# Transposing queries and keys before they are split, with three smaller changes of order, in one diffusion trunk layer

## The chip, the cores and the metric

The kernel runs on one core of a Trainium2 chip. The core has five engines that run their own instruction queues and meet at semaphores: TensorE (PE in the profile; PEld is its weight load), VectorE (DVE), ScalarE (ACT), GpSimd (POOL), and SyncE (SP), which here only issues transfers. The metric is the device time of one execution in microseconds; the median of several runs is given.

## The reference

One trunk layer is computed for 256 prompt tokens and 1024 latent tokens of width 1024, in fp32:

```
h = rms_norm(x) * (1 + sc1) + sh1          # sc, sh, g from an adaLN of the conditioning
z = h @ w_in                               # 5376 columns
  q, k = per-head RMSNorm (8 query heads, 2 key heads of 64); latents also get 2-D rotary positions
  attention: latents read 512 cached keys + 1024 latent keys, the prompt reads itself
  HGRN2: gated linear recurrence, both directions, 4 heads of 128
merged = sigmoid(g0) * (o_h @ w_ho) + sigmoid(g1) * (o_a @ w_ao)
x = x + g1 * (merged @ w_out)
h = rms_norm(x) * (1 + sc2) + sh2
x = x + g2 * (square(relu(h @ w_ff1)) @ w_ff2)
y = rms_norm(x) * final_norm_w
```

It returns y for prompt and latents, the prompt's normalised keys and its values, and the final recurrent states.

## The kernel before

**Split products.** PE multiplies in a reduced format (fp32r) at a higher rate than plain fp32. For accuracy each operand is split into a high half (a copy rounded to fp32r, made by ACT) and a low half (the rest, subtracted by DVE); a product is then three matmuls: high x high, high x low, low x high. The helper is `split` at L276 to L278, so L277 is always ACT's copy and L278 always DVE's subtraction, whatever the tile. Queries and keys are stacked: a tile of 128 partitions holds 64 rows of the high half over 64 of the low half, so that one matmul with a key tile that holds its high half twice, and one with its low half twice, give the score (L699).

**Stages, in order of time.** (1) Conditioning and the input's norm, then queries of the second group of heads, keys and values: for each of three token tiles (512, 512 and 256 tokens) and each of eight 128-wide slices of the width, the input is transposed (`norm1_tr`, L256), scaled into high and low halves (`norm1_col`: L265 and L270 on ACT, L271 on DVE), and multiplied (`front_z`, L563, L564, L567). (2) Queries of the first group (`z_tok`). (3) Attention, with other columns of w_in as filler between its steps. (4) The recurrence, with the merge gates as filler. (5) Branch outputs, merge, output projection. (6) The first FFN product of the prompt (L1361 to L1383, matmuls L306 to L308): 16 pairs of 128 columns; beside it the sums of the latents are made (`sums1`, L1343). (7) The first FFN product of the latents, with a scheme of seven block products instead of eight (L1442 on); the sums of products are taken by DVE. (8) The second FFN product, in seven chains, the last one P3, and the final norm, whose last blocks come after the chain.

**Queries and keys (L383 to L487).** When a pair of 128-token blocks is projected, `qk_norm` normalises it and, for latents, rotates it. `k_stack` and `q_consume` then split each block in token order (`kst` L419/L420, `qst` L473/L474), and put a function `late` on a list. `late` transposes four 128 x 128 pieces on PE (L425, L479), copies the PSUM tile out on ACT (`kT` L428, `qT` L482) and stores it to scratch memory (KS, QS), from where attention loads K and Q tiles (`Kl`, `Ql`). For keys both halves are written twice, so that each tile is loaded whole. `kT` and `qT` share a ring of two buffers (G); normalised queries and keys lie in rings of three (D, E); the split copies have a ring of four (B). The PSUM ring `t` has two buffers and serves the input's transposes and these.

**What sets the order.** PE's instructions run in the order in which they are written. When a `late` runs is decided by `due` and `flush`: a small clock of DVE's work, to which each item adds a constant (`DUE`), against one of PE's; `flush` is called between steps of PE. From stage 6 on SP is in written order too. The order of ACT, DVE and POOL (and SP before) is written by the framework's planner, which simulates the program by its own cost estimates and gives a free engine the ready instruction that is earliest in the program. `tc.high_priority(offset=n)` makes it count n places earlier. The order is then fixed for the run. In stage 6 a weight block of 1 MB comes into one of two buffers (`wraw`), is split by `w_oc` under offset 150 into a ring of six (`wsp`), and the product is squared by `relu2` under offset 400.

**The last norm.** `square` sums the squares of half a row block on ACT (L1675); `final` (L1677) forms the reciprocal root with POOL (L166) and scales each half by it and by the norm's weight in one DVE instruction (L1685), then stores it.

## Time and profile before

| what | value |
|---|---|
| median of 3 runs | 2084.43 us (2083.12 to 2084.66) |
| profiled execution, its own time | 2085.25 us |
| its span | 2083.5 us |
| granted TensorE clock, mean | 0.995 |
| PE busy | 97% of the span |

The profile gives for each group of instructions the line of the program, the engine, the tiles as out<-in, their shape and count, the busy time and mean duration, and the idle time of the engine just before them with what ended it. In the order of time a row begins with its start and its duration in us. A matmul's duration contains its latency; matmuls overlap, so the price of one is read from start to start.

### The profile page before, as it was taken

Reading aid. Unit: us, or ns where it says so; the run is one execution under the profiler, and the core shown is the slowest. Engines: PE = TensorE matmul, PEld = TensorE weight load, DVE = VectorE, ACT = ScalarE, POOL = GpSimd, SP = SyncE. Lnnn points to the kernel's source line nnn. Section 1 sums busy time; section 2 is a strip of 40 time slices with the busy share of each in tenths; the row PEclk is TensorE's granted clock in tenths of the full one; section 3 lists DMA queues with packets and bytes.
Section 4 is the critical chain, followed back from the end, with each engine's and each line's share of the span. In section 5 each row is a group of like instructions: output and inputs, shape, how many; then the busy total and the mean of one; then the engine's idle time right before and its main releaser. Section 6 shows DMA issues by size and latency. Waiting matters only on the chain.

```text
span 2083.5 us, 33949 instructions
## 1 busy us (share of the span) xinstructions
PE 2026.9 (97%) x12552; PEld 1747.1 (84%) x12552; DVE 1405.9 (67%) x2677; ACT 943.1 (45%) x1928; POOL 539.3 (26%) x577
## 2 busy tenths in 40 slices
PE   6899999999999999999999999999999999999998
PEld 5688889988899878888888888988888888888886
DVE  4784776777776788779354636776666666677786
ACT  4754555555555522222231425654555444333442
POOL 1472233432332355546112100222221210000010
PEclk9999999999999999999999999999999999999999
DMA  9464221241222255445644523764444479545773
GB/s 309 125 195 139 71 73 55 66 133 53 68 82 70 73 168 181 129 151 166 220 132 147 192 101 110 228 198 160 144 155 153 153 260 366 161 155 176 232 249 128
DMA packets 230246, 319.24 MB, mean 153 GB/s; under 512 B 18072, under 2 KB 148720, under 8 KB 230080
## 3 DMA queue, kind: packets, MB, share of 16 engines
q1 hardware_dynamic: 217664, 277.41, 41.4%
q0 software_dynamic: 12416, 39.66, 5.4%
q8 instruction: 99, 1.62, 0.3%
q14 instruction: 67, 0.55, 0.1%
HBM read 229.43 MB, written 87.57 MB: 152 GB/s over the span
## 4 chain that ended last, share of the span: by engine, by line
PE 84%; DVE 8%; DMA 3%; ACT 3%; issue 2%; POOL 1%; SPq 0%; DVEq 0%; POOLq 0%; ACTq 0%
PE ps_g L306 7%; PE ps_g L308 7%; PE ps_g L307 7%; PE ps_s L699 4%; PE ps_t L740 4%; PE ps_g L1593 2%; PE ps_g L1591 2%; PE ps_g L1592 2%; PE ps_s L1439 2%; PE ps_g L756 2%; PE ps_s L1441 2%; PE ps_s L1440 2%; PE ps_g L755 2%; PE ps_g L323 2%; PE ps_g L325 2%; PE ps_g L324 2%
## 5 line engine op out<-in xcount | busy, mean ns | idle before, releaser
L306 PE MATMUL ps_g<-hs,wsp 128*128 128x512 f32 (+1 forms) x896 | 323.5, 361 | 0.4 <-DVE adas L186 0.4
L308 PE MATMUL ps_g<-hs,wsp 128*128 128x512 f32 (+1 forms) x896 | 310.8, 347 | 0.8 <-DVE wsp L278 0.8
L307 PE MATMUL ps_g<-hs,wsp 128*128 128x512 f32 (+1 forms) x896 | 310.6, 347 | 0.0
L718 POOL TENSOR_SCALAR pexp<-pexp,rs 128x512 f32<-128x512 f32 (+1 forms) x104 | 170.6, 1647 | 363.0 <-ACT pTh L743 180.0
L277 ACT ACTIVATE wsp<-wraw 128x1024 fp32r<-128x1024 f32 x110 | 109.6, 998 | 260.5 <-PE ps_g L307 82.9
L278 DVE TENSOR_TENSOR wsp<-wraw,wsp 128x1024 fp32r<-128x1024 f32 x110 | 133.6, 1216 | 120.3 <-ACT wsp L277 120.0
L308 PEld LDWEIGHTS ps_g<-hs,wsp 128*128 128x128 f32 x896 | 170.2, 190 | 22.8 <-DVE wsp L278 1.0
L306 PEld LDWEIGHTS ps_g<-hs,wsp 128*128 128x128 f32 x896 | 170.2, 190 | 21.6 <-issue 4.8
L307 PEld LDWEIGHTS ps_g<-hs,wsp 128*128 128x128 f32 x896 | 170.7, 190 | 15.3
L743 ACT ACTIVATE pTh<-ps_t 128x512 fp32r<-128x512 f32 x200 | 118.8, 601 | 131.0 <-PE ps_t L740 126.7
L700 DVE TENSOR_REDUCE mx<-ps_s 128x1 f32<-128x512 f32 (+1 forms) x208 | 136.9, 663 | 49.6 <-PE ps_s L699 48.8
L277 ACT ACTIVATE ah<-ar 128x640 fp32r<-128x640 f32 (+1 forms) x112 | 81.0, 723 | 190.3 <-PE ps_g L1592 102.3
L710 ACT ACTIVATE pexp<-ps_s,ngm 128x512 f32<-128x512 f32 (+1 forms) x208 | 137.3, 669 | 42.4 <-DVE ngm L704 40.7
L278 DVE TENSOR_TENSOR ah<-ar,ah 128x640 fp32r<-128x640 f32 (+1 forms) x112 | 90.2, 805 | 81.1 <-ACT ah L277 80.4
L744 DVE TENSOR_TENSOR pTl<-ps_t,pTh 128x512 fp32r<-128x512 f32 x200 | 136.1, 681 | 11.9 <-ACT pTh L743 11.4
L699 PE MATMUL ps_s<-Kl,Ql 128*128 128x512 f32 (+1 forms) x416 | 127.8, 412 | 2.5 <-ACT pexp L710 2.5
L740 PE MATMUL ps_t<-ident,pexp 128*128 128x128 f32 x800 | 121.0, 273 | 2.5 <-DVE pexp L718 1.5
L323 PE MATMUL ps_g<-wsp,hs 128*128 128x256 f32 x400 | 117.1, 293 | 0.0
L325 PE MATMUL ps_g<-wsp,hs 128*128 128x256 f32 x400 | 113.4, 283 | 0.0
L324 PE MATMUL ps_g<-wsp,hs 128*128 128x256 f32 x400 | 113.0, 283 | 0.0
L756 PE MATMUL ps_g<-pTl,Vl 128*128 128x256 f32 x400 | 105.4, 286 | 4.0 <-DVE pTl L744 3.9
L755 PE MATMUL ps_g<-pTh,Vl 128*128 128x256 f32 x400 | 105.5, 284 | 1.3 <-DVE oa L765 1.0
(420 smaller groups left out, 5425.3 us busy)
## 6 DMA issues: line engine op xcount, KB each, us to landing
ar<-AF SPq DMA_DIRECT2D x112, 320.0 KB, 3.4
wraw<-in_w_ff SPq DMA_DIRECT2D x32, 1024.0 KB, 6.2
wr<-in_w_ff SPq DMA_DIRECT2D x128, 256.0 KB, 4.4
wraw<-in_w_in SPq DMA_DIRECT2D x18, 1024.0 KB, 5.9
wraw<-in_w_ada SPq DMA_DIRECT2D x16, 1024.0 KB, 5.5
AF<-a POOLq DMA_DIRECT2D x48, 256.0 KB, 2.7
AF<-t POOLq DMA_DIRECT2D x48, 256.0 KB, 2.3
wa<-in_w_ada SPq DMA_DIRECT2D x32, 256.0 KB, 5.8
```

The source lines that it names most:

```text
L277: s_.activation(hi, raw, AF.Copy)
L278: v.tensor_tensor(lo, raw, f32(hi), op=ALU.subtract)
L306: pe.matmul(out, hi[:, k, :], mh, start=(first and k == 0), stop=False)
L307: pe.matmul(out, hi[:, k, :], ml, start=False, stop=False)
L308: pe.matmul(out, lo[:, k, :], mh, start=False, stop=(last and k == kcs - 1))
L323: pe.matmul(po[:, bb, :], mh[:, off:off + P], wh[:, k % 4, :], start=(k == 0), stop=False)
L324: pe.matmul(po[:, bb, :], mh[:, off:off + P], wl[:, k % 4, :], start=False, stop=False)
L325: pe.matmul(po[:, bb, :], ml[:, off:off + P], wh[:, k % 4, :], start=False, stop=(k == KC - 1))
L699: pe.matmul(pq[:, 0:n], self.qh[:, q0:q0 + P], K[self.g][var][self.kts[i]], start=(var == 0), stop=(var == 1))
L718: NORM[(i + j) % len(NORM)].tensor_scalar(x, x, self.rs[j], None, op0=ALU.mult)
L740: pe.transpose(pt[:, a, j * P:(j + 1) * P], self.Ps[j][i][:, b * P:(b + 1) * P], ident)
L755: pe.matmul(pv[:, 0:256], V[self.g][kg][:, b, :], hi[:, a, :], start=(k == 0), stop=False)
```

## The change

Four things are changed.

1. Queries and keys are no longer split and stacked in token order. `late` transposes the plain fp32 tile (for a pair of blocks: four transposes for queries, two heads of 64 in each; two for keys, both key heads in each) into PSUM, and splits there: ACT copies the high half, DVE subtracts the low half from PSUM. Key halves are stored once. The loads of K and Q put the two halves together: two transfers of 64 partitions each. There is one `late` per pair where there was one per block, and the constants of `DUE` become 3.4 and 4.4.
2. In stage 6 the weight splits get an offset of 500 instead of 150.
3. In stage 7 the sum `u2` gets an offset of 100.
4. For the second half of the five row blocks that end last, POOL multiplies by the norm's weight ahead, in place, after the half's squares are summed (in chain P3). `final` then only scales this half by the reciprocal root, on ACT.

```diff
-    QS = [[DR((P, 4, n), "QS%d_%d" % (g, t)) for t, (_, n, _) in enumerate(TT)] for g in range(2)]
+    QS = [[DR((2, 2, P, n), "QS%d_%d" % (g, t)) for t, (_, n, _) in enumerate(TT)] for g in range(2)]
-    KS = [DR((P, 4, KG[kg]), "KS%d" % kg) for kg in range(4)]
+    KS = [DR((2, P, KG[kg]), "KS%d" % kg) for kg in range(4)]
...
     def k_stack(kr, kgv, pos):
-        st = S((P, 2, 2, 2, 64), F32R, name="kst")
-        kb = kr.unsqueeze(2).broadcast_to([P, 2, 2, 64])
-        s_.activation(st[:, :, 0], kb, AF.Copy)
-        v.tensor_tensor(st[:, :, 1], kb, f32(st[:, :, 0]), op=ALU.subtract)
         def late():
-            pt = PS("t", (P, 4, P))
-            for j in range(4):
-                pe.transpose(pt[:, j, :].bitcast(F32R), st[:, j // 2, j % 2].rearrange("p a d -> p (a d)"), ident_r)
-            e = S((P, 4, P), F32R, name="kT")
+            pt = PS("t", (P, 2, P))
+            for b in range(2):
+                pe.transpose(pt[:, b, :], kr[:, b].rearrange("p k d -> p (k d)"), ident)
+            e = S((P, 2, 256), F32R, name="kT")
             with tc.high_priority(offset=600):
-                s_.activation(e, pt, AF.Copy)
-            dma(KS[kgv][:, :, pos * P:(pos + 1) * P], e)
+                split(e[:, 0], e[:, 1], pt.rearrange("p b c -> p (b c)"))
+            dma(KS[kgv][:, :, pos * P:(pos + 2) * P].rearrange("v p n -> p v n"), e)
...
+            t, off = pr // 2, (pr % 2) * 256
+            def late():
+                pt = PS("t", (P, 2, 256))
+                for b in range(2):
+                    for a in range(2):
+                        pe.transpose(pt[:, a, b * P:(b + 1) * P], qr[:, b, 2 * a:2 * a + 2].rearrange("p h d -> p (h d)"), ident)
+                hi, lo = [S((P, 2, 256), F32R, name="qT") for i in range(2)]
+                with tc.high_priority(offset=600):
+                    split(hi, lo, pt)
+                for i, x in enumerate((hi, lo)):
+                    dma(QS[g][t][i, :, :, off:off + 256].rearrange("a p n -> p a n"), x)
+            pending.append((due(DUE[1]), late))
...
-    DUE = (2.2, 2.6, 6.5)
+    DUE = (3.4, 4.4, 6.5)
...
                 x = S(dt=F32R, name="Ql")
-                dma(x, QS[self.g][self.t][:, h % 4, :])
+                for i in range(2):
+                    dma(x[64 * i:64 * i + 64, :], src[i, a, r:r + 64, :])
...
-            K[g][var][kg] = S((P, KG[kg]), F32R, name="Kl")
-            dma(K[g][var][kg], KS[kg][:, 2 * g + var, :])
+            x = K[g][var][kg] = S((P, KG[kg]), F32R, name="Kl")
+            for i in range(2):
+                dma(x[64 * i:64 * i + 64, :], KS[kg][var, 64 * g:64 * g + 64, :])
...
-            with tc.high_priority(offset=150 if i > 1 else 0):
+            with tc.high_priority(offset=500 if i > 1 else 0):
                 wt = w_oc(r, half)
...
-        v.tensor_tensor(u2, Y, s1_, op=ALU.add)
+        with tc.high_priority(offset=100):
+            v.tensor_tensor(u2, Y, s1_, op=ALU.add)
...
-            v.scalar_tensor_tensor(x, x, rst[:, 0:1], fw[0][:, c], op0=ALU.mult, op1=ALU.mult)
+            if i in ready.get(b, ()):
+                s_.activation(x, x, AF.Copy, scale=rst[:, 0:1])
+            else:
+                v.scalar_tensor_tensor(x, x, rst[:, 0:1], fw[0][:, c], op0=ALU.mult, op1=ALU.mult)
...
+    ready = {}
+    def weigh(b, i):
+        x = xt[b][:, i * 512:(i + 1) * 512]
+        g_.tensor_tensor(x, x, fw[0][:, i * 512:(i + 1) * 512], op=ALU.mult)
+        ready.setdefault(b, []).append(i)
+    def square_weigh(b, i):
+        square(b, i)
+        weigh(b, i)
...
-    chain2("P3", Z, False, {2 * j + 4: lambda b=b: square(b, 1) for j, b in enumerate((4, 5, 6, 7, 9))})
+    chain2("P3", Z, False, {2 * j + 4: lambda b=b: square_weigh(b, 1) for j, b in enumerate((4, 5, 6, 7, 9))})
```

More of the change, by code (lines that the diff above doesn't have):

```diff
@@ L462, in kv_consume @@
         v_stack(vr, 2, kgv, pos)
-        for b in range(2):
-            k_stack(kr[:, b], kgv, pos + b)
+        k_stack(kr, kgv, pos)
     def q_consume(g):
@@ L468, in f @@
             _, qr = qk_norm(po.rearrange("p b (h d) -> p b h d", h=4), 4, qwb, 2 * pr, pr < 4)
-            for b in range(2):
-                blk = 2 * pr + b
-                t, off = blk // 4, (blk % 4) * P
-                st = S((P, 4, 2, 64), F32R, name="qst")
-                s_.activation(st[:, :, 0], qr[:, b], AF.Copy)
-                v.tensor_tensor(st[:, :, 1], qr[:, b], f32(st[:, :, 0]), op=ALU.subtract)
-                def late(st=st, t=t, off=off):
-                    pt = PS("t", (P, 4, P))
-                    for h in range(4):
-                        pe.transpose(pt[:, h, :].bitcast(F32R), st[:, h].rearrange("p a d -> p (a d)"), ident_r)
-                    e = S((P, 4, P), F32R, name="qT")
-                    with tc.high_priority(offset=600):
-                        s_.activation(e, pt, AF.Copy)
-                    dma(QS[g][t][:, :, off:off + P], e)
-                pending.append((due(DUE[1]), late))
+            t, off = pr // 2, (pr % 2) * 256
[10 more added lines that the diff above has]
+            pending.append((due(DUE[1]), late))
         return f
@@ L495, in cache_kv @@
             v_stack(cv[:, 2 * b:2 * b + 2], 2, 0, 2 * b)
-        for b in range(4):
-            k_stack(ck[:, b], 0, b)
+        for b in range(0, 4, 2):
+            k_stack(ck[:, b:b + 2], 0, b)
     clk = {"pe": 0.0, "dve": 0.0}
-    DUE = (2.2, 2.6, 6.5)
+    DUE = (3.4, 4.4, 6.5)
     def due(work):
@@ L777, in load_k @@
             x = S((P, 2, 256), F32R, name="Kl")
-            dma(x, KS[3][:, 2 * g:2 * g + 2, :])
+            for i in range(2):
+                dma(x[64 * i:64 * i + 64], KS[3][:, 64 * g:64 * g + 64, :].rearrange("v p n -> p v n"))
             K[g][0][3], K[g][1][3] = x[:, 0, :], x[:, 1, :]
```

6 lines of the change are left out of this document (4 added, 2 removed), and 2 rows, old and new, of the table RING_OF.

## The prediction

> **What bounds the kernel now.** I read the page first, then busy time by stretch, then TensorE's waits, then the order of time where those waits lie.
>
> ```profile
> span 2083.5 us, 33949 instructions
> ...
> PE 2026.9 (97%) x12552; PEld 1747.1 (84%) x12552; DVE 1405.9 (67%) x2677; ACT 943.1 (45%) x1928; POOL 539.3 (26%) x577
> ```
>
> TensorE (PE) is the bound nearly everywhere, so an edit pays in two ways only: fewer PE slots, or a shorter PE wait. The stretches that the edits touch:
>
> ```profile
> 92.00:112.00 20.00, 15.53 (x82) 11.74 (x80) 15.76 (x38) 16.04 (x41) 11.63 (x17) 1.00 0.51 156
> 112.00:176.00 64.00, 64.00 (x468) 59.46 (x469) 38.90 (x77) 33.54 (x75) 30.94 (x33) 1.00 0.68 208
> ...
> 1310.00:1340.00 30.00, 26.90 (x220) 26.28 (x219) 24.08 (x41) 17.20 (x33) 8.31 (x11) 1.00 0.73 227
> ...
> 1384.00:1400.00 16.00, 14.21 (x63) 11.43 (x62) 14.13 (x26) 6.81 (x12) 2.82 (x4) 1.00 0.39 118
> ```
>
> After the window come its length and the busy time of PE, weight loads, VectorE (DVE), ScalarE (ACT) and GpSimd (POOL). In 92 to 112 us, where the prompt's part of the first projection runs, PE lacks 4.5 us and ACT is busy 16 of 20; from 112 to 176 PE never rests, so there only fewer slots count. The first FFN product of the prompt lacks 3.1 us in 1310 to 1340, its hand-over to the latents 1.8 in 1384 to 1400. Who ended PE's waits (total, times, longest):
>
> ```profile
> PE ps_t L938 <- DVE usf L909: 5.7, 3, 3.0
> ...
> PE ps_s L308 <- DVE wsp L278: 2.3, 2, 1.5
> ...
> PE ps_s L1439 <- DVE u L1453: 1.8, 1, 1.8
> PE ps_s L567 <- DVE hs L271: 1.7, 1, 1.7
> ...
> PE ps_g L308 <- DVE wsp L278: 0.8, 1, 0.8
> ...
> PE ps_t L425 <- ACT qT L482: 0.5, 1, 0.5
> ```
>
> and, of the stretch 76 to 112 us alone, the group of the input's transposes:
>
> ```profile
> L256 PE MATMUL ps_t<-ident,xr 128*128 128x128 f32 x20 | 4.0, 292 | 3.4 <-ACT xnb L270 2.3 <-ACT kT L428 1.2
> ```
>
> **Transposes, PE slots.** Before, a pair of token blocks costs eight transposes of split data (fp32r) for four query heads, and eight for the keys. After, four and two of plain fp32. The keys have 7 pairs (2 cached, 5 new), the queries 10 (5 per group of heads): 136 transposes become 54. The price is read from start to start, in order of time, plain fp32 first:
>
> ```profile
> 69.78 0.60 PE L256 MATMUL ps_t<-ident,xr 128*128 128x128 f32 x4
> 70.13 0.48 PE L563 MATMUL ps_g<-wraw,hs 128*128 128x512 f32 x1
> 70.44 0.40 PE L564 MATMUL ps_g<-wsp,hs 128*128 128x512 f32 x1
> 70.68 0.40 PE L563 MATMUL ps_g<-wraw,hs 128*128 128x512 f32 x1
> ```
>
> ```profile
> 105.27 0.46 PE L479 MATMUL ps_t<-ident,qst 128*128 128x128 f32 x4
> 105.57 0.46 PE L563 MATMUL ps_s<-wsp,hs 128*128 128x512 f32 x1
> 105.87 0.39 PE L564 MATMUL ps_s<-wsp,hs 128*128 128x512 f32 x1
> ```
>
> Four plain ones take 0.35 us, and the product behind them 0.31 where the next has 0.24: 0.42 in all. Four split ones take 0.30, the product behind 0.30: 0.36. A query pair goes from 2 x 0.36 = 0.72 to 0.42, saving 0.30; a key pair from 0.72 to 0.35/2 + 0.07 = 0.25, saving 0.47. That is 10 x 0.30 + 7 x 0.47 = 6.3 us. Where two groups or another transpose follow one another, the 0.06 behind a group was paid once or not at all; on slots alone it is 10 x 0.25 + 7 x 0.42 = 5.5. I take 5.9, the middle.
>
> The Trainium skill's FP8 and Floating Point Precision (TensorE Precision Notes) speaks against this part: true fp32 takes four passes through the array. The two fences above disagree for transposes: the plain kind costs 0.35 against 0.30 for four. What four passes would do to the time is a rival below.
>
> **Transposes, other engines.** Per key or query pair:
>
> ```profile
> L428 ACT ACTIVATE kT<-ps_t x14: 587/598/689, 76.7 to 138.5; 128x512 fp32r<-128x512 f32 x14
> ...
> L419 ACT ACTIVATE kst<-qa x8: 408/416/539, 78.0 to 116.4; 128x256 fp32r<-128x256 f32 x8
> ```
>
> ```profile
> L482 ACT ACTIVATE qT<-ps_t x20: 580/598/713, 89.5 to 173.7; 128x512 fp32r<-128x512 f32 x20
> ```
>
> ```profile
> L474 DVE TENSOR_TENSOR qst<-qa,qst x16: 414/426/1509, 85.7 to 156.7; 128x256 fp32r<-128x256 f32 x16
> ```
>
> ```profile
> L744 DVE TENSOR_TENSOR pTl<-ps_t,pTh x200: 670/680/693, 192.3 to 732.7; 128x512 fp32r<-128x512 f32 x100
> ```
>
> ```profile
> 91.89 0.38 ACT L443 ACTIVATE kve<-ps_g 128x256 f32<-128x256 f32 x1 [0.60 <-PE ps_g L567]
> ```
>
> ACT paid 2 x (0.42 + 0.60) = 2.0 us a pair. After, one copy out of PSUM: 0.60 for a query pair, 0.38 for a key pair. DVE paid 2 x 0.43 and pays 0.68 (queries) or about half of that (keys), now reading PSUM. So ACT loses about 1.4 x 10 + 1.6 x 7 = 25 us, DVE 2 + 3.6 = 5.6. Off the path this is worth nothing; it counts where PE waits for ACT, in 76 to 112 us: 2.3 (xnb) + 1.2 (kT) + 0.5 (L425 behind qT) = 4.0 us. With some four pairs handled there, ACT's 16 us fall by about 6, more than the whole wait. The 1.7 us before L567 are DVE's and stay for the larger part. Against this stands a longer turn of the PSUM buffer: two rings serve the input's transposes and these, and a turn now ends with DVE's subtraction behind ACT's copy. I take 3.0 us gained; bounds 0 and 5.7 (all rows named).
>
> What also moves: normalised queries and keys stay in their 3 buffers until PE transposes them, where the split copies had 4 of their own, so the next pair's rotation on DVE and POOL can come later; and K and Q tiles are loaded as two halves of 64 partitions. Loads go from 34 to 68, key stores from 14 to 7: 27 more issues on SP.
>
> ```profile
> L699 PE MATMUL ps_s<-Kl,Ql x416: 274/393/501, 177.7 to 718.6; 128*128 128x512 f32 x128, 128*128 128x256 f32 x11
> L101 SPq DMA_DIRECT2D Ql<-QS x20: 319/320/1123, 148.3 to 708.0; - x20
> ```
>
> At 0.32 us each that is 8.6 us of SP over 560 us. The first Q load is issued 29 us before its first use; that is the cover. I put it at nothing; without the cover, each of the 20 Q loads would add one issue, 6.4 us. The altered due times (3.4 and 4.4 for a pair against 2.2 and 2.6 for a block) only choose between which products PE does the transposes.
>
> **Weight splits first (L1365).** Two PE waits of this stage are a late low half:
>
> ```profile
> 1306.68 1.08 ACT L277 ACTIVATE wsp<-wraw 128x1024 fp32r<-128x1024 f32 x1
> ```
>
> ```profile
> 1310.92 0.69 DVE L278 TENSOR_TENSOR hs<-xa,form 128x512 fp32r<-128x512 f32 x1
> 1311.52 1.23 DVE L278 TENSOR_TENSOR wsp<-wraw,wsp 128x1024 fp32r<-128x1024 f32 x1
> ```
>
> ```profile
> 1326.69 8.90 DMA wraw<-in_w_ff
> ```
>
> The high half was ready at 1307.8, yet DVE did sums for the latents' product until 1311.5. But these sums stand later in the program than the split, which already had an offset of 150. The planner took them because by its own clock the split was not ready; a higher rank does not change that. What the 500 does change is ACT, where splits now go before the squared ReLU (offset 400): high halves come up to one such pair earlier. The third wait is a weight load of 8.9 us, issued when DVE freed its buffer. Of 2.3 + 0.8 = 3.1 us I take 1.2; bounds 0 and 3.1. The delayed ReLU holds one of six PSUM buffers 1.1 us longer, of products that take 24 x 26.9/220 = 2.9 each: nothing.
>
> **The sum ahead (L1453).**
>
> ```profile
> 1389.15 0.39 PE L1441 MATMUL ps_s<-hs,wsp 128*128 128x512 f32 x1
> ```
>
> ```profile
> 1395.44 0.68 DVE L1325 TENSOR_TENSOR hs<-xa,hs 128x512 fp32r<-128x512 f32 x1
> 1396.04 0.68 DVE L1453 TENSOR_TENSOR u<-ps_s,s 128x512 f32<-128x512 f32 x1
> ```
>
> Its product ended at 1389.5, DVE reached it at 1396.0, after splits (L1325) that also stand later in the program. The same doubt holds, with the same caution: 0.7 of 1.8 us; bounds 0 and 1.8. What it passes (the T4 splits) is needed two products later.
>
> **The last norm.**
>
> ```profile
> 2062.24 0.69 DVE L1655 TENSOR_TENSOR y<-ps_g,g2b 128x512 f32<-128x512 f32 x1 [7.74 <-PE ps_g L1593]
> ...
> 2078.80 1.42 DVE L1685 SCALAR_TENSOR_TENSOR x<-x,frst,fwb 128x512 f32<-128x512 f32 x2 [0.73 <-POOL frst L166]
> ```
>
> ```profile
> 2076.97 0.63 ACT L1675 ACTIVATE jk<-x 128x512 f32<-128x512 f32 x1 [5.29 <-DVE x L1661]
> ```
>
> ```profile
> 2079.58 0.99 SPq L101 DMA_DIRECT2D out_y_prompt<-x  x2
> ```
>
> Only the last block is exposed; the others are normalised while PE makes its products. ACT's scaling (0.63 by its square of that size) runs beside DVE's first half, so the second store follows the first after 0.33 us of issue instead of 0.66: 0.3 gained, bounds 0 and 0.7. The five multiplications on POOL fall into the last chain. One takes about 1.3:
>
> ```profile
> 86.85 1.31 POOL L412 TENSOR_TENSOR qa<-qa,qb 128x512 f32<-128x512 f32 x1 [0.79 <-DVE qa L405]
> ```
>
> While it ran, a subtraction that takes 0.43 took 1.51 (the longest of L474). So they can hold DVE's splits by 5 x 1.3 = 6.5 us. DVE had done its last split of the chain 7.7 us before PE was through (the idle time of L1655); that covers it, and with the cover gone it would cost those 6.5.
>
> **Sum.** 5.9 + 3.0 + 1.2 + 0.7 + 0.3 = 11.1 us. The profiled run took 2085.25, 1.75 beyond its span and 0.8 above the median of 2084.43. From the profiled run it is 2074.1, from the median 2073.3; I say **2073.5**. The best ends of all terms give 6.3 + 5.7 + 3.1 + 1.8 + 0.7 = 17.6, the worst 5.5: 2067 to 2079, this case's own range.
>
> **Rivals.**
> 1. Only PE slots are saved; the waits for ACT become waits for DVE behind it, and the ranks change nothing: 5.9 + 0.3 gives 2078.2. For it: DVE is as busy as ACT in 92 to 112 (15.8). Against: DVE loses work too.
> 2. The order that the planner writes for DVE, ACT and SP shifts through attention and the recurrence, since PE's filler work is dealt out from another point. One more wait like the 5.7 us before L938, with a few of 1 us, takes 9 us: 2082.5.
> 3. Slower: the longer PSUM turn in 76 to 112 us. Some nine turns (2 of cached keys, 4 of new keys, 3 of queries) each hold the next input transpose by 0.68, and by 1.3 more if POOL blocks the subtraction: 9 x 2.0 = 18 in place of the 3.0 gained: 2094. It makes the kernel slower from (2088.6 - 2076.5)/9 = 1.3 us a turn. Against: L744, which reads PSUM, never took over 693 ns beside POOL's work, while L474, with both inputs in SBUF, did.
> 4. Four passes: 54 x 0.30 + 17 x 0.07 = 17.4 us against 136 x 0.075 + 34 x 0.06 = 12.2 now, so 5.2 lost instead of 5.9 gained: 2084.6. Rows at 69.78 speak against it.
> 5. All waits named go: 2066.
>
> The Trainium skill's SBUF — State Buffer (Who interferes with whom) has the same split as rival 3's last sentence: DVE and GpSimd exclude each other for a whole instruction, and of DVE's plain operations those with two SBUF inputs. By that rule the new subtraction is free of POOL and a turn costs 0.68, so rival 3 ends near 2082; L744's row agrees.
>
> **How the numbers follow.** What can be told from no change is about 0.2%, 4.2 us: 2080.2 to 2088.6. Chances: forecast 0.48, rival 1 0.22, rival 2 0.14, rival 3 0.07, rival 4 0.04, rival 5 0.05. Faster: 0.48 + 0.05 + 0.18 of rival 1 + 0.03 of rival 2 = 0.74. Slower: rival 3 and 0.02 of rival 2 = 0.09. The same: 0.17. The range 2065 to 2083.5 leaves out half of rival 2, rivals 3 and 4: some 0.18.
>
> **What would show it.** The rows of the new transposes: four from start to start near 0.35, two near 0.18; if 0.6, rival 4. In 92 to 112 us the waits for xnb and kT gone, ACT under 12; if rows "PE ps_t L256 <- DVE" stand there instead, rival 1 or 3. The waits of L308 and L1439: whether DVE's order has changed. At the end the second prompt store right behind the first. Wrong it would be made above all by new PE waits between 180 and 1000 us, which no edit touches.

## The result, and the profile after

The changed kernel takes 2071.62 us (median of 4 runs, 2070.82 to 2072.94) against 2083.77 us (4 runs, 2080.06 to 2084.66): a ratio of 0.9937, 95% interval 0.9924 to 0.995. That is 12.2 us less; 2073.5 had been said. In the experiments further down, one run of 3788 us and one of 9775 us, far outside the others of their kernels, are left out of the medians. The profiled execution took 2071.04 us, 1.8 beyond its span. The page of the changed kernel begins:

```profile
span 2069.2 us, 33722 instructions
...
PE 2016.9 (97%) x12470; PEld 1737.3 (84%) x12470; DVE 1404.0 (68%) x2655; ACT 924.4 (45%) x1882; POOL 550.0 (27%) x582
```

Busy time by stretch, in the columns of the prediction; the third and fourth stretch answer to 1310 to 1340 and 1384 to 1400 before, since everything there now lies 16 us earlier:

```profile
92.00:112.00 20.00, 19.06 (x118) 16.58 (x118) 18.86 (x47) 13.71 (x34) 14.29 (x19) 1.00 0.81 245
112.00:176.00 64.00, 63.51 (x437) 56.93 (x436) 43.99 (x78) 24.73 (x55) 33.68 (x34) 1.00 0.55 175
1294.00:1324.00 30.00, 26.78 (x218) 26.09 (x217) 23.85 (x40) 17.56 (x33) 8.30 (x11) 1.00 0.69 217
1368.00:1384.00 16.00, 13.77 (x57) 10.95 (x56) 14.79 (x27) 7.76 (x15) 2.82 (x4) 0.94 0.33 101
```

The front is fuller (PE 19.06 of 20, was 15.53), though the first stretch now holds 7.7 us of the work behind it, since the projection ends at 104.3; ACT is busy 13.7 us there, not under 12. The two stretches that the ranks were to fill are as they were: 26.78 of 30 (26.90), 13.77 of 16 (14.21). In the last one the granted clock, third column from the right, is 0.94. The waits of TensorE say the same:

```profile
PE ps_g L751 <- DVE pTl L739: 6.8, 10, 1.5
...
PE ps_t L936 <- DVE usf L907: 3.3, 3, 2.2
PE ps_s L1437 <- DVE u L1452: 2.2, 1, 2.2
...
PE ps_s L308 <- DVE wsp L278: 1.8, 2, 1.5
...
PE ps_g L308 <- DVE wsp L278: 1.4, 1, 1.4
```

and of 76 to 112 us alone there are left:

```profile
PE ps_t L256 <- DVE kT L278: 1.2, 2, 0.8
PE ps_t L256 <- ACT xnb L270: 0.9, 1, 0.9
```

That is 2.1 us of the 5.7 that stood there before; the 1.7 before L567 have no successor. The waits for a low half of the prompt's weights (L308) are 3.2 us, were 3.1; the one for the u2 sum is 2.2, was 1.8. Attention waits longer for pTl (6.8, was 3.9, as the row below has it for the kernel before), the recurrence less for usf (3.3, was 5.7).

```profile
PE ps_g L756 <- DVE pTl L744: 3.9, 7, 1.1
```

Where the span lost its 14.3 us, by the last (or first) matmul of a stage in the order of time, in us:

| stretch | before | after | difference | of it clock |
|---|---|---|---|---|
| to the end of the front projection (L567, now L559) | 111.95 | 104.32 | -7.6 | -1.7 |
| to the last filler product beside attention (L325) | 623.6 | 620.9 | -2.7 | -1.7 |
| to the last product of the recurrence (L949, now L947) | 276.2 | 270.2 | -5.9 | -3.4 |
| to the first of the latents' first FFN product | 372.2 | 372.4 | +0.2 | 0 |
| latents' first FFN product | 306.9 | 309.0 | +2.1 | +1.7 |
| the second FFN product | 384.6 | 384.6 | 0 | 0 |
| behind the last matmul | 8.1 | 7.8 | -0.3 | |

The last column counts the slices at half clock that a stretch has more or fewer than before, at the 1.7 us each that is worked out below. It comes to 5 of the 14 us. The records of the granted clock know two values here, 1.0 and 0.5, and change only on a grid of 3.41 us that stays in place through an execution. Busy time by such slices, the kernel before (the window, its length, PE, weight loads, DVE, ACT, POOL, granted clock):

```profile
737.39:740.80 3.41, 1.20 (x8) 1.07 (x8) 3.32 (x8) 0.51 (x1) 2.55 (x4) 1.00 0.71 222
740.80:744.21 3.41, 3.41 (x10) 2.63 (x8) 3.38 (x6) 0.09 (x1) 3.41 (x4) 0.50 1.09 355
890.99:894.40 3.41, 1.41 (x9) 1.27 (x10) 3.41 (x6) 0.60 (x1) 3.41 (x5) 1.00 0.47 173
894.40:897.81 3.41, 3.41 (x9) 2.26 (x7) 3.37 (x7) 0.00 (x0) 0.45 (x1) 0.50 0.00 0
```

and the same view of the changed kernel:

```profile
1378.57:1381.98 3.41, 1.18 (x6) 0.71 (x5) 3.41 (x8) 1.54 (x2) 1.31 (x2) 1.00 0.14 43
1381.98:1385.39 3.41, 3.41 (x10) 2.63 (x9) 0.84 (x1) 0.00 (x0) 0.00 (x0) 0.50 0.93 248
...
876.81:880.22 3.41, 2.02 (x11) 1.79 (x12) 3.41 (x5) 0.60 (x1) 3.24 (x4) 1.00 0.35 124
880.22:883.64 3.42, 3.42 (x43) 2.54 (x43) 3.38 (x8) 0.00 (x0) 0.00 (x0) 1.00 0.02 7
```

A slice in which PE is busy 1.2 or 1.4 of 3.41 us is followed by one at half clock, which costs 3.41/2 = 1.7 us of work; one with 2.02 is not. The pauses that empty the slices of 890.99 and of 876.81 are the same, before the same transposes, and of the same length (2.2 us); only the grid fell otherwise. Over the profiles of all kernels here, slices at full clock with PE busy up to 1.5 us were always followed by a half, those with 1.9 or more never, those between sometimes. From the front projection to the last matmul, slices at half clock follow the pauses at 727, 737 and 891 us before; after, there is only the one that follows the wait for u2.

The Trainium skill's TensorE: Matmul & The Clock Gate (What's actually happening) describes such a window, 4096 cycles at 1.2 GHz or 3413 ns, free-running; the grid of 3.41 us agrees. Its rule of thumb (HAM oscillation) is that idle gaps beyond about 3.4 us bring the clock down; here a gap of 2.2 us, lying within one slice, does it.

### The profile page after: what moved, and what is told of

Read it like the earlier page. It is cut to its first block, busy times and chain, and to the rows that moved or that the text cites. A ratio compares the mean times of both kernels' runs of the same rounds, so it can differ in the third digit from the quotient of the medians.

```text
span 2069.2 us, 33722 instructions
## 1 busy us (share of the span) xinstructions
PE 2016.9 (97%) x12470; PEld 1737.3 (84%) x12470; DVE 1404.0 (68%) x2655; ACT 924.4 (45%) x1882; POOL 550.0 (27%) x582
## 4 chain that ended last, share of the span: by engine, by line
PE 80%; DVE 8%; DMA 4%; ACT 2%; issue 2%; POOL 1%; POOLq 0%; ACTq 0%; DVEq 0%
PE ps_g L306 6%; PE ps_g L308 6%; PE ps_g L307 6%; PE ps_s L694 4%; PE ps_t L735 3%; PE ps_g L1592 2%; PE ps_g L1590 2%; PE ps_g L1591 2%; PE ps_s L1437 2%; PE ps_s L1438 2%; PE ps_s L1439 2%; DMA wraw<-in_w_ff 2%; PE ps_g L751 2%; PE ps_s L1590 2%; PE ps_s L1592 2%; PE ps_s L1591 2%
## 5 line engine op out<-in xcount | busy, mean ns | idle before, releaser
L308 PE MATMUL ps_g<-hs,wsp 128*128 128x512 f32 (+1 forms) x896 | 309.5, 345 | 1.4 <-DVE wsp L278 1.4
L278 DVE TENSOR_TENSOR wsp<-wraw,wsp 128x1024 fp32r<-128x1024 f32 x110 | 134.9, 1228 | 122.3 <-ACT wsp L277 122.0
L308 PEld LDWEIGHTS ps_g<-hs,wsp 128*128 128x128 f32 x896 | 169.3, 189 | 23.2 <-DVE wsp L278 1.6
L278 DVE TENSOR_TENSOR ah<-ar,ah 128x640 fp32r<-128x640 f32 (+1 forms) x112 | 91.9, 822 | 79.1 <-ACT ah L277 78.0
L694 PE MATMUL ps_s<-Kl,Ql 128*128 128x512 f32 (+1 forms) x416 | 130.4, 411 | 0.9 <-ACT pexp L705 0.7
L325 PE MATMUL ps_g<-wsp,hs 128*128 128x256 f32 x400 | 112.9, 282 | 0.0
L750 PE MATMUL ps_g<-pTh,Vl 128*128 128x256 f32 x400 | 105.2, 283 | 1.4 <-DVE um L892 0.7
```

What stands on the lines that cost most here:

```text
L278: v.tensor_tensor(lo, raw, f32(hi), op=ALU.subtract)
L308: pe.matmul(out, lo[:, k, :], mh, start=False, stop=(last and k == kcs - 1))
L694: pe.matmul(pq[:, 0:n], self.qh[:, q0:q0 + P], K[self.g][var][self.kts[i]], start=(var == 0), stop=(var == 1))
```

## The experiments

Each kernel was timed beside the kernel before on the same chip; the ratios are to that. The median of the kernel before was 2083.85, 2084.34 and 2084.62 us in the three sets, so a difference between kernels of different sets can be off by a microsecond or so.

### The three parts by themselves

The transposes alone are the changed kernel with the other edits undone:

```diff
-            with tc.high_priority(offset=500 if i > 1 else 0):
+            with tc.high_priority(offset=150 if i > 1 else 0):
...
-        with tc.high_priority(offset=100):
-            v.tensor_tensor(u2, Y, s1_, op=ALU.add)
+        v.tensor_tensor(u2, Y, s1_, op=ALU.add)
...
-    chain2("P3", Z, False, {2 * j + 4: lambda b=b: square_weigh(b, 1) for j, b in enumerate((4, 5, 6, 7, 9))})
+    chain2("P3", Z, False, {2 * j + 4: lambda b=b: square(b, 1) for j, b in enumerate((4, 5, 6, 7, 9))})
```

> The unsplit transposes alone; offsets and last norm are as before. Theory A (the prediction's terms hold): 5.9 of slots and 3.0 of waits, 8.9 us below the kernel before, and the rest of the 14 us comes from the other edits. Theory B (read from the two traces): all that was gained up to 1000 us is this part's, some 16 us, and the other edits give back about 2: so 13 to 16 us below the kernel before, that is at or up to 2 us below the changed kernel. In the trace theory B wants the end of the front projection near 104.3 and the first recurrence product about 14 us earlier than before; the waits of the prompt's first FFN product unchanged, since no rank touches them here.

Measured: 2072.55 us (median of 4 runs, 2069.46 to 2076.74), ratio 0.9946 (0.9933 to 0.996). In the profile the front projection ends at 105.20, the first recurrence product comes 13.3 us earlier than before, and the last matmul 15.6 us. The gain is 11.3 us, with an interval of 8.3 to 14.0, so the time decides neither for theory A's 8.9 nor for theory B's 13 to 16. The trace looks like theory B: 14.1 us are gained up to the recurrence's end. But this profile has four slices fewer at half clock than that of the kernel before, which is 6.8 us, and without them the 15.6 are 8.8, theory A's sum. Beside this part, about 1 us of the whole gain is left for the two ranks and the norm, less than the intervals can tell.

The ranks alone, and the norm alone, are the kernel before with

```diff
-            with tc.high_priority(offset=150 if i > 1 else 0):
+            with tc.high_priority(offset=500 if i > 1 else 0):
...
-        v.tensor_tensor(u2, Y, s1_, op=ALU.add)
+        with tc.high_priority(offset=100):
+            v.tensor_tensor(u2, Y, s1_, op=ALU.add)
```

and with

```diff
+            if i in ready.get(b, ()):
+                s_.activation(x, x, AF.Copy, scale=rst[:, 0:1])
+            else:
                 v.scalar_tensor_tensor(x, x, rst[:, 0:1], fw[0][:, c], op0=ALU.mult, op1=ALU.mult)
...
+        g_.tensor_tensor(x, x, fw[0][:, i * 512:(i + 1) * 512], op=ALU.mult)
```

> The two ranks alone (500 for the weight splits, 100 for the u2 sum); all else is as before. Theory A: 1.2 + 0.7 = 1.9 us below the kernel before. Theory B: the order on DVE hardly changes, so the waits of L308 stay near 3 us and the one before L1439 near 1.8 us, and the time is within 1 us of before; should the wait before that product come out above 2 us as in the changed kernel, the granted clock falls behind it and the time is up to 2 us above before. Either way everything up to 1280 us keeps its times within 0.5 us.

> The last norm alone: second halves multiplied ahead on GpSimd, scaled on ScalarE. Theory A and theory B agree on 0.3 us (0 to 0.7) below the kernel before: the second prompt store is issued about 0.2 to 0.3 earlier behind the last product. A rival: the five multiplications hold up DVE's splits in the last chain (up to 6.5 us); then PE waits for DVE would stand in the last 25 us that the kernel before does not have.

Measured: ranks 2084.19 us, ratio 1.0 (0.9991 to 1.0009); norm 2085.44 us, ratio 1.0005 (0.9996 to 1.0014). The ranks leave the waits standing; of the kernel with the ranks alone:

```profile
PE ps_s L308 <- DVE wsp L278: 1.9, 2, 1.5
...
PE ps_s L1439 <- DVE u L1454: 1.2, 1, 1.2
...
PE ps_g L308 <- DVE wsp L278: 0.8, 1, 0.8
```

That is 2.7 us before L308, where five profiles without the rank have 2.3 to 3.7. The u2 wait of 1.2 is no effect of the rank either: without it, it is 1.0 to 2.6 in five profiles, with it 0.5 to 2.2 in six. Of the norm the two last stores show what was said: in the kernel with the norm alone they end 4.96 us behind the last matmul, 5.15 in the kernel before and in the one with the transposes alone. 0.2 us is there, far below what the time can show.

### The price of a plain transpose

Each of the 54 new transposes is issued twice:

```diff
                 pe.transpose(pt[:, b, :], kr[:, b].rearrange("p k d -> p (k d)"), ident)
+                pe.transpose(pt[:, b, :], kr[:, b].rearrange("p k d -> p (k d)"), ident)
...
                         pe.transpose(pt[:, a, b * P:(b + 1) * P], qr[:, b, 2 * a:2 * a + 2].rearrange("p h d -> p (h d)"), ident)
+                        pe.transpose(pt[:, a, b * P:(b + 1) * P], qr[:, b, 2 * a:2 * a + 2].rearrange("p h d -> p (h d)"), ident)
```

> The changed kernel, with each of the 54 new plain fp32 transposes issued twice on TensorE (the second overwrites the first with the same values). It measures a transpose's price by itself. Theory A and B: 54 x 0.0875 = 4.7 us above the changed kernel where PE is the bound throughout, somewhat less where part of it falls into a wait (3.5 to 4.7). Four passes for each (rival 4, 0.30 a transpose): 16 us. A shift of the order that the planner writes would show as waits between 180 and 1000 us that the changed kernel does not have, and adds or takes some 5 us beside it.

Measured: 2081.59 us, ratio 0.9986 (0.9977 to 0.9995), 10.0 above the changed kernel; neither number. A group of the changed kernel, in the order of time, and then one of this kernel:

```profile
108.34 0.60 PE L470 MATMUL ps_t<-ident,qa 128*128 128x128 f32 x4
108.69 0.36 PE L323 MATMUL ps_g<-wsp,hs 128*128 128x256 f32 x1
108.89 0.28 PE L324 MATMUL ps_g<-wsp,hs 128*128 128x256 f32 x1
```

```profile
133.73 0.27 PE L471 MATMUL ps_t<-ident,qn 128*128 128x128 f32 x1
133.84 0.27 PE L472 MATMUL ps_t<-ident,qn 128*128 128x128 f32 x1
...
134.49 0.27 PE L472 MATMUL ps_t<-ident,qn 128*128 128x128 f32 x1
134.52 0.36 PE L323 MATMUL ps_g<-wsp,hs 128*128 128x256 f32 x1
134.72 0.28 PE L324 MATMUL ps_g<-wsp,hs 128*128 128x256 f32 x1
```

From start to start a transpose takes 0.107 us, except the last before a product (0.03, with 0.08 more behind the product): four take 0.35, eight 0.79. The doubling adds 0.44 to each of 10 query pairs and 0.21 (0.35 against 0.14 for the last two key pairs) to each of 7 key pairs: 5.9 us. The other 4 are, as far as is known, waits and clock: the profile has 1.7 us before L471 for POOL's rotation, and the mean granted clock of the runs is 0.9964 where the changed kernel has 0.9973, worth 1.9 us. So the price is 0.107 in a row, not 0.0875, and rival 4's 0.30 is out.

### The clock

Two pauses of the kernel before are filled with matmuls that nobody reads (`fill` is 10 for unit 0 of the recurrence, 8 for unit 13, and 0 for the others):

```diff
             kt = self.kt = PS("t", (P, 4, P))
+            for i in range(self.fill):
+                pe.matmul(kt, ident_r, ident_r.unsqueeze(1).broadcast_to([P, 4, P]), start=True, stop=True)
```

> The kernel before, with matmuls that nobody reads (identity by identity, 512 columns) on TensorE ahead of the transposes of units 0 and 13 of the recurrence: 10 and 8 of them, 2.3 and 1.8 us at the full clock, where TensorE pauses 3.3 and 2.4 us. Theory C (the granted clock is set slice by slice, 3.41 us each, and a slice in which TensorE works less than about 1.35 us is followed by one at half clock, which costs 1.7 us): the pauses are still as long for the data, but the stretches at half clock behind them (740.8 and 894.4 in the kernel before) are gone: 2 x 1.7 = 3.4 us below before in the profile, 2 to 3.4 in the median, since the grid falls elsewhere in each execution. Rival D (the clock falls because of the wait itself, or of power, not of an idle array): the half-clock stretches stay, and the time is that of before or up to 1 us longer.

Measured: 2084.41 us, ratio 0.9999 (0.9989 to 1.0009). In its profile, in the order of time (L938 is the filler, L940 the transposes behind it):

```profile
740.06 2.59 PE L938 MATMUL ps_t<-ident 128*128 128x512 f32 x10
743.62 0.66 PE L940 MATMUL ps_t<-ident,usf 128*128 128x128 f32 x4 [0.97 <-DVE usf L909]
...
892.13 2.00 PE L938 MATMUL ps_t<-ident 128*128 128x512 f32 x8
894.43 0.66 PE L940 MATMUL ps_t<-ident,usf 128*128 128x128 f32 x4 [0.30 <-DVE usf L909]
```

No slice between 103 and 1399 us is at half clock; the slices that hold the two pauses have PE busy 2.44 us or more. The recurrence, from the last filler product of attention to its own last product, takes 272.3 us; three profiles of that same program part have 273.9 with one slice at half clock and 275.5 and 276.2 with two. That is some 1.7 us a slice, and fits theory C as to the mechanism: a slice with too little work brings the clock down, and work that nobody reads fills it. The time does not show it. The mean granted clock of the runs rose from 0.9951 (23 runs before) to 0.9961 (12 runs), worth 2 us, but the median is the same, to within 2.1 us either way. In the profile the front took 1.8 us longer than before, attention 1.7, and a wait of 2.6 us for u2 brought a half slice that the profile of before does not have. Whether that is scatter or the filler's doing stays open.

### The u2 sum and the weight splits, by an order that binds

If the rank does not move the sum, an edge in the issue order does:

```diff
-            v.tensor_tensor(u2, Y, s1_, op=ALU.add)
+            u2_sum = v.tensor_tensor(u2, Y, s1_, op=ALU.add)
...
-            for kb in range(4):
-                fsplit("T4", kb, xa[0][kb + 4])
+            with tc.issue_after(u2_sum.ins):
+                for kb in range(4):
+                    fsplit("T4", kb, xa[0][kb + 4])
```

> The changed kernel, with VectorE's T4 splits queued behind the first u2 sum by an edge in the issue order instead of a rank. Theory A (the prediction: the sum's place in DVE's queue is what costs, the rank only failed to move it): the sum starts about 4 us earlier, the 2.2 us wait of L1437 goes, and with it the stretch at half clock behind it (1.7 us): 2.2 to 4 us below the changed kernel in its profile, 2 to 3 in the median. Rival B (the T4 splits are then late themselves): a wait for them of up to 2 us before the last product of that step, and nothing is gained.

Measured: 2070.22 us, ratio 0.9927 (0.9909 to 0.9945). In DVE's order of time the changed kernel has, and this kernel has:

```profile
1379.80 0.68 DVE L1323 TENSOR_TENSOR hs<-xa,hs 128x512 fp32r<-128x512 f32 x1
1380.40 0.68 DVE L1452 TENSOR_TENSOR u<-ps_s,s 128x512 f32<-128x512 f32 x1
```

```profile
1379.18 0.68 DVE L1452 TENSOR_TENSOR u<-ps_s,s 128x512 f32<-128x512 f32 x1
1379.78 0.42 DVE L1322 CAST hs<-xa 128x512 fp32r<-128x512 f32 x1
```

The sum now stands ahead of the T4 splits, 3.7 us earlier when counted from the first matmul of the stage. In the profile the latents' first product takes 304.7 us in place of 309.0: the wait (2.4, from start to start of the matmuls on both sides of it, less one slot) and the half slice behind it (1.7) are gone, 4.1 us, with no wait for T4 instead. The median fell by 1.4, and the intervals overlap, so the size in the time is open; the mechanism of the prediction's term is right, its lever (the rank) was wrong.

The same for the sums of the latents' product, behind the low halves of the weights:

```diff
                 wt = w_oc(r, half)
+            low[i] = tc.nc.cur_bb.bb.instructions[-1]
...
-            sums1((i - 3) // 3, (i - 3) % 3)
+            with tc.issue_after(low[max(3, i - 3)]):
+                sums1((i - 3) // 3, (i - 3) % 3)
```

> As e5_u2, and besides the sums for the latents' first product are queued on VectorE behind low halves of the prompt's weights that stand up to three steps ahead of them (by an edge in the issue order). Theory A: the 3.2 us of waits of L308 fall by 1.5 to 3, and the time comes out 1.5 to 3 below e5_u2. Rival G (VectorE has too little room in that stage: what is held back is missed later): waits for form or hs stand at the start of the latents' product, and the time is that of e5_u2 or up to 5 us above.

Measured: 2064.97 us, ratio 0.9908 (0.9891 to 0.9926); 5.3 below the kernel of the edge for u2 alone. The waits of L308 are gone, and no new one stands at the latents' product:

```profile
1296.00:1326.00 30.00, 29.90 (x249) 29.70 (x249) 27.52 (x46) 21.90 (x42) 6.80 (x9) 1.00 0.76 236
1370.00:1386.00 16.00, 16.00 (x74) 13.29 (x73) 15.72 (x28) 6.94 (x12) 3.00 (x4) 1.00 0.28 86
```

PE works 29.90 of 30 us where it worked 26.78. From the output projection (L1275) to the latents' product the profile has 210.8 us in place of 214.5. That is theory A, by 3.7 us of it; the rest of the 5.3 is within the interval.

Both edges together with eight filler matmuls before unit 13:

> As e8_sums, with 8 matmuls that nobody reads ahead of the transposes of unit 13 (as in e6_fill). Theory C: the stretch at half clock near 883 is gone, the pause of 2.4 us before those transposes is filled; 1.7 us below e8_sums where its grid fell badly and nothing where it did not, so 0.5 to 1.7 below in the median, which the interval will hardly tell. Rival D: the stretch stays.

Measured: 2065.4 us, ratio 0.9905 (0.9892 to 0.9917), an interval that lies below the changed kernel's. No slice after 63 us is at half clock until behind the last matmul, where the kernel without the filler has one at 883, as theory C had it. The wait before the transposes of the recurrence is down to

```profile
PE ps_t L938 <- DVE usf L907: 1.4, 3, 0.8
```

in place of 3.3. Against the kernel without the filler the time is the same (0.4 us above, where 0.5 to 1.7 below had been expected), so that the filler gains time is not shown. These two are the fastest kernels of the study, some 6 us below the changed one.

### The due times

```diff
-    DUE = (3.4, 4.4, 6.5)
+    DUE = (2.2, 2.6, 6.5)
```

in the changed kernel; the other way, `(4.4, 5.2, 6.5)`; and in the kernel before `(1.7, 2.2, 6.5)` in place of `(2.2, 2.6, 6.5)`.

> The changed kernel, with the due times of before (2.2 and 2.6 in place of 3.4 and 4.4). They decide only between which products the transposes and all filler behind them stand. Theory E (what was gained between 112 and 1000 us beyond the slots is a matter of where the planner puts the work and of where the clock's grid falls): the front projection ends within 1 us of 104.3, the waits of L751, L735 and L936 come out different by some us in all, and the time is within 5 us of the changed kernel on either side, mostly above. Rival F (the longer due times are themselves what brings the gain): the front projection ends 3 us or more later and the time is 5 us or more above the changed kernel.

> The changed kernel with due times of 4.4 and 5.2 for a pair, that is twice those that the kernel before has for a block (2.2 and 2.6), in place of 3.4 and 4.4. Theory H (a due time only has to be long enough that VectorE and GpSimd have a pair ready; the short ones left TensorE waiting 10.7 us for one pair): no long wait of a transpose, and the time is within 3 us of the changed kernel. Rival I (3.4 and 4.4 are a narrow optimum): later transposes hold up the next pairs' buffers, waits of 3 us or more stand in 76 to 180 us, and the time is 4 us or more above it.

> The kernel before with due times of 1.7 and 2.2 for a block, half of what the changed kernel has for a pair. Theory A: the due times are no gain by themselves; a block's transposes come earlier than its split is ready, waits of L425 and L479 grow, and the time is that of before or up to 5 us above. Rival K (the earlier filler is what shortens the front projection): it ends 3 us or more before 112 and the time is 3 us or more below.

Measured: 2089.03 us, ratio 1.0021 (1.001 to 1.0032); 2083.96 us (2075.33 to 2087.76), ratio 0.9992 (0.9982 to 1.0002); and 2090.96 us, ratio 1.0034 (1.0021 to 1.0046). With the short times the changed kernel is slower than the kernel before (by 4.7 us), and 17.4 us slower than with its own times. Theory E is out and rival F holds: the front projection ends at 109.8, 5.4 us later, and most of the rest is one transpose right behind it. The wait, in the table of waits and in the order of time:

```profile
PE ps_t L470 <- POOL qa L412: 14.1, 4, 10.7
```

```profile
120.45 1.11 PE L470 MATMUL ps_t<-ident,qa 128*128 128x128 f32 x4 [10.69 <-POOL qa L412]
```

PE's queue came to the transposes of a pair while POOL and DVE were still rotating it, and stood 10.7 us, then ran on at half clock. Of the kernel before with shorter times, the same by its own names:

```profile
PE ps_t L479 <- DVE qst L474: 6.6, 2, 4.6
```

It is 6.3 us slower than the kernel before, a little beyond theory A's bound, and its front ends at 111.5, so rival K is out: shorter times are no gain by themselves. With the long times, in the changed kernel, no transpose waits for long; the scores of attention do, for ACT's exponentials (9.0 us, 0.7 in the changed kernel):

```profile
PE ps_s L694 <- ACT pexp L705: 9.0, 6, 4.2
```

The longest of them stands where attention begins, in the order of time:

```profile
179.20 1.06 ACT L277 ACTIVATE wsp<-wraw 128x1024 fp32r<-128x1024 f32 x1 [5.53 <-DMA wraw<-in_w_in]
181.97 1.88 DVE L695 TENSOR_REDUCE mx<-ps_s 128x1 f32<-128x512 f32 x3
184.96 2.08 PE L694 MATMUL ps_s<-Kl,Ql 128*128 128x512 f32 x4 [4.20 <-ACT pexp L705]
```

The first scores were done at 176.9, but in DVE's queue the split of a weight block stood before their maxima. SP had issued the load of that block at 172.57, between the stores of the last query pairs, and ACT had to wait for it until 179.20. What set back the other exponentials was not traced. Theory H falls; rival I's size came true, 12.3 us, and its place only nearly (181 to 185 us, behind the pairs' stores, not at their buffers in 76 to 180).

Of the three pairs of due times tried, 3.4 and 4.4 is the best by 12 us. And 4.4 and 5.2 for a pair are what the kernel before has for two blocks: with the due times carried over unchanged, all the edits together show no gain (0.9982 to 1.0002).

### ScalarE's relief

In the changed kernel ScalarE is given back what it lost, with copies that nobody reads:

```diff
+    def spare(src):
+        x = S((P, 4, P), name="spare")
+        for b in range(2):
+            s_.activation(x[:, 2 * b:2 * b + 2], src[:, b], AF.Copy)
+        return x
...
+        x = spare(kr.rearrange("p b k d -> p b (k d)").unsqueeze(2).broadcast_to([P, 2, 2, P]))
...
+            x = spare(qr.rearrange("p b (j h) d -> p b j (h d)", j=2))
...
                     split(hi, lo, pt)
+                    s_.activation(x, x, AF.Copy)
```

> The changed kernel with ScalarE's saving undone: for each pair three copies that nobody reads, two of 128x256 where the kernel before split (0.42 each) and one of 128x512 behind the split of the transposes (0.6); TensorE's transposes and VectorE's work stay as changed. Theory A (3.0 of the front's gain is relief of ScalarE, the waits for xnb, kT and qT): the waits of L256 for ACT come back and the front projection ends 2 to 4 us later than in the changed kernel, near 107. Rival J (the gain is fewer TensorE slots and a better order alone): it ends within 1 us of 104.3. The scatter of the later stages (one or two stretches at half clock of 1.7 us) applies to both.

Measured: 2075.4 us, ratio 0.9947 (0.9935 to 0.9959), above the changed kernel by 3.8 us in the median and by 2.1 in the ratio, with intervals that overlap. ACT is busy 943.6 us again, 943.1 in the kernel before and 924.4 in the changed one. The front projection ends at 106.30. That is 2.0 later than in the changed kernel, but four other profiles with the changed kernel's front have it between 105.2 and 106.4. The waits that theory A named did not come back; from 76 to 112 us this kernel has

```profile
PE ps_t L256 <- DVE kT L278: 2.0, 2, 1.1
PE ps_t L256 <- ACT xnb L270: 0.8, 1, 0.8
```

so 2.8 us in place of 2.1, and the 0.7 are DVE's. In attention the scores (L694's place) wait 2.7 us for ACT's exponentials in place of 0.7. The end of the front does not decide between the two numbers; but that ScalarE's relief took the waits for xnb away is not borne out: they stay away with its work put back.

## Why the prediction was right, and where it was not

The time was 1.9 us from the number, and the sign and the main place (the front) were right. That it came so near is in part luck, as the terms that follow show: one term brought nothing, and a part of the gain stood in no term. By its own steps:

**Slots: 5.9 us, about right.** Two plain transposes stand 0.21 us apart from the next group, four 0.35, as the two lines of the changed kernel show (0.35 at 108.34 above, and):

```profile
75.50 0.38 PE L421 MATMUL ps_t<-ident,ck 128*128 128x128 f32 x2
75.71 0.60 PE L256 MATMUL ps_t<-ident,xr 128*128 128x128 f32 x4
```

From start to start, a group of four split transposes took 0.29 us, so the 34 groups of the kernel before some 9.9 us; the 17 groups now take 5.2, waits left out. The product behind a group takes 0.07 to 0.08 longer than the next, 23 times before and 10 times now, another 0.8. Together that is 5.5 us. The range for one, between 0.0875 and rival 4's 0.30, is settled at 0.107 in a row; the 0.0875 was a group's mean with the cheap last one in it.

**Waits in the front: 3.0 us, the size about right, the cause not.** Of the 5.7 us that stood in 76 to 112 us, 3.6 went. But the step said that the waits for xnb, kT and qT (4.0) would go by ACT's relief and the 1.7 before L567 "stay for the larger part". The latter went whole, in the kernel that gives ACT its work back too; the 4.0 became 2.1, of which 1.2 are now DVE's low half of kT, as rival 1 had it; and what did go for xnb stays away when ACT is loaded again. That DVE's saving (the step's own 5.6 us) or the fewer turns of the PSUM rings are behind it is argued only; no run undid either. DVE's saving was also smaller than said: in the kernel with the transposes alone DVE is busy 2.2 us less than before (1403.7 against 1405.9), while ACT is busy 21.1 less (922.0 against 943.1), near the 25 of the step. So what took the waits away stays open.

**The due times: put at nothing, the largest miss.** The step said that they "only choose between which products PE does the transposes". The same edit with the numbers of before (2.2 and 2.6, now for a pair) is 17.4 us slower than with the new ones, and with twice those, the same time for two blocks, 12.3: the whole gain. The choice of a place in PE's written order is a price: too early, PE stands in front of a pair that is not rotated; too late, attention waits. The total came out because the value in the diff is a good one, which nothing in the sum said; that is luck. It is also rival 2's mechanism: a shift of the order through attention costs some 10 us, as that rival put it; it came true with the neighbouring constants, and not with these.

**The ranks: 1.2 + 0.7 us, measured as nothing.** The time says so to within 1.9 us, and the waits stand as they were. The step had the reason in hand (the planner takes what its clock has ready, and a rank does not change that) and then took some 40% of the wait all the same. The two edges show that the waits were real and worth 2.4 + 3.7 us in the profile, and that the rank is not what moves them.

**The loads: put at nothing, rightly.** SP's issues took longer than the 0.32 us of the step (median 0.53 for Ql, 0.59 for Kl), but no matmul of the changed kernel waited for a K or Q tile.

**The last norm: 0.3 us, of which 0.2 came.** The two halves are now scaled side by side, and the stores follow each other (0.81 us for both, was 0.99). In the order of time of the changed kernel:

```profile
2064.79 0.72 ACT L1685 ACTIVATE x<-x,frst 128x512 f32<-128x512 f32 x1 [1.11 <-POOL frst L166]
2064.79 0.75 DVE L1687 SCALAR_TENSOR_TENSOR x<-x,frst,fwb 128x512 f32<-128x512 f32 x1 [0.73 <-POOL frst L166]
2065.57 0.81 SPq L101 DMA_DIRECT2D out_y_prompt<-x  x2
```

DVE's splits were not held up by 6.5 us; the wait for ah is 1.0 us in the kernel with the norm alone, 0.4 before and after.

**What the sum lacked: the clock.** All terms counted a pause at its own length. A pause that left a slice of 3.41 us with less than about 1.5 us of work cost another 1.7 here. In the profile before, that was 5.1 us between 727 and 898 (and 1.7 at the start of the front), among them behind the wait of L938 that rival 2 names; in the profile after it was 1.7, behind the wait for u2. The profiled pair thus overstates the change. The mean granted clock is 0.9953 over 27 runs of the kernel before (those of the first set of experiments) and 0.9973 over the 4 of the changed one; what is missing from 1, times the span, is some 9.9 us lost against 5.7. So about 8 of the 12.2 us are work and waits, and about 4 the clock. The sum's 11.1 without the 1.9 of the ranks is 9.2, near those 8. The total came near because the clock, which the sum lacked, made up for what the ranks did not bring.

**The rivals.** "PE ps_t L256 <- DVE kT L278" stands in the table, as either wanted, with 1.2 us over two turns, not nine turns of 2.0. Rival 3's doubt, whether POOL would block the new subtractions, is settled by their row in the changed kernel:

```profile
L278 DVE TENSOR_TENSOR qT<-ps_t,qT x10: 674/687/692, 87.1 to 156.7; 128x512 fp32r<-128x512 f32 x10
```

Five of these ten, and five of the seven for keys (408 to 424 ns), ran beside an instruction of POOL, and none took longer for it. Rival 1 was right on the ranks and on kT, and wrong that nothing else would go. Rival 4 is refuted by the slots, and rival 5 by the waits that remain (its 2066 is also 1 us below the 2067 to which the best ends of the sum add). The trust in 180 to 1000 us was half right: pTl waits 2.9 us more in attention, and 2.4 less for usf in the recurrence.

## What to carry to other kernels

A constant that places work in a written order is a term of the sum like any instruction: read in the trace when the operand is ready and when the consumer's queue arrives, on both sides of the place, before costing it at nothing. A scheduling rank moves work only among what the planner holds ready; where its clock and the chip's differ, an explicit order edge does what the rank does not (here 2.4 and 3.7 us of waits). And a pause of TensorE that leaves a clock slice with less than 1.5 us of work can cost half a slice more than its length, so read the granted clock behind each long wait, and do not take one profile's slices for the kernel's.

## What was not expected of the hardware

The granted clock is set in slices of 3.41 us on a grid whose phase differs from execution to execution. A pause of 2.2 us before the same transposes was followed by a half-clock slice in the profile before (slice 890.99: PE 1.41 busy) and not in the changed kernel's (876.81: 2.02). In a half slice a 512-column matmul takes 0.43 us from start to start in place of 0.23. With matmuls on data that nobody reads issued into the pause, no half slice followed in the three places where this was tried (slices at 740 and 890 us of one kernel, 879 of another, PE busy 2.44 us or more); as the changed kernel shows, some such pauses have none without them either. And a plain fp32 transpose of 128 x 128 costs 0.107 us in a row, 1.9 times a quarter of a 512-column fp32r matmul (0.227/4). Four of them take 0.35 us before a product, where four of split data took 0.29.
